# Modulation vectors of a layered model: summed along rows of transposed weights instead of across partitions

## The chip, the cores and the metric

One core of one Trainium2 chip runs the whole program as one launch. The metric is the device time of that core in microseconds (us). A difference is told as after against before.

## The reference, cut to what matters

A 256 x 1024 activation passes through a first block (gated recurrence, spatial gating, SwiGLU), then a gated linear attention layer ("GLA"), a retrieval layer ("PEER"), a sliding-window attention layer and a second PEER layer. Everything is float32. Each of these layers is modulated by vectors that depend on a conditioning vector `c` alone:

```python
mod = (jax.nn.silu(c) @ w_mod[l] + b_mod[l]).reshape(bsz, N_MOD, D_MODEL)      # first block, 6 parts
mod = c_act @ mod_w[l] + mod_b[l]                                              # two later layers, 6 parts each
sh1, sc1, g1, sh2, sc2, g2 = jnp.split(mod, 6, axis=-1)
kv_mod = c_act @ kv_mod_w + kv_mod_b                                           # 2 parts
h = rmsnorm(x, g) * (1.0 + scale) + shift                                      # shift, scale: parts 0, 1, 3, 4
x = x + gate * y                                                               # gate: parts 2 and 5
```

Each part is a vector of 1024 numbers, the product of a vector of 1024 and a 1024 x 1024 weight matrix (4 MB). The kernel computes 18 of the parts in the way that is changed here: parts 2 to 5 of the first block (key "m"), 0 to 5 of the two later layers ("m0", "m1") and two for the shared keys and values ("kv"). Parts 0 and 1 of the first block are made by other code (`mod_start`), which stays.

## The kernel before, in words

The weights of all layers stream from HBM as tiles of 128 x 1024 float32 (512 KB) into a ring of buffers called `raw`. `raw()` (L225) issues the load on the queue of SyncE (SP). For the layers, `halves()` splits each tile in two: ScalarE (ACT) copies it to a rounded type (`wh`, L268) and VectorE (DVE) subtracts (`wl`, L270). TensorE (PE) then makes three products for each block: `wh` by the activation's high part (L284 and its like), `wl` by the same (L285), `wh` by the low part (L286). There are 3 `wh` and 3 `wl` buffers, and some stages add more with `more()`. In PEER, 128 tiles of `peer_u` are multiplied first (L1617 to L1619), then 128 tiles of `peer_v` (L284 to L286), for which `acth` and `actl` are made as well (L1713, L1714).

The modulation parts are background work. `mod_part` is a generator that yields after each of its 8 weight tiles. `pump()` is called after every tile that `halves()` gives, and advances the generator by one unit each time its credit, raised by `s.rate` (0.2 to 0.75), reaches 1. `need()` runs a part to its end where a layer wants it, and `mod()` and `gate()` fetch it. A unit goes like this: one `raw` tile holds two row blocks of 512 columns, and DVE adds each, times its number of silu(c), to an accumulator:

```python
rj = r[:, j * 512:j * 512 + 512]
if k == 0:
    i = nc.vector.tensor_scalar(acc, rj, c[:, 0:1], None, op0=OP.mult)                                     # L383
else:
    i = nc.vector.scalar_tensor_tensor(acc, rj, c[:, k:k + 1], acc, op0=OP.mult, op1=OP.add)               # L385
```

After 4 units (half a part) the 128 partitions of `acc` (tile `modacc`, one buffer) hold partial sums. Four products with a vector of ones on PE (L391, 8 passes) sum them across the partitions into PSUM, DVE adds a bias (L395, tile `modsb`), GpSimd (POOL) writes the 512 numbers to a DRAM row (L397), and, for parts that are no gates, reads them back as columns (L399). POOL also loads the bias for each half (L376). Gates stay in DRAM until `gate()` loads them, repeated over 128 partitions, on SP. `scale_vec` (L550) is the first reader of the column form.

The order on each engine isn't the order of the code: the framework's planner places the instructions by its own costs and priorities, and adds the semaphores. An engine then runs its list in order, so that an instruction which waits holds up all behind it.

At the start, `warm()` (L328) runs 18 dummy products on a zeroed tile (`modbias`, L164) while the first loads land. In the GLA layer, L1183 multiplies the query with the running state of each chunk of 64 rows, with a tile of zeros as the state of the first chunk, and L1185 adds the product within the chunk.

Of the kernel before, what the change touches and what calls it, by code (L numbers as in the profile page):

```python
# [9 lines left out]
F32 = mybir.dt.float32  # L10
# [30 lines left out]
COLS = [("c", 8), ("cx", 8), ("c2", 8), ("g_mix", 8), ("g_ffn", 8), ("bm", 16), ("lb", 16), ("b_s", 4)]  # L41
COLS2 = [("ng", 32), ("kvg", 8), ("bg2", 4)]
# [69 lines left out]
class Prog:  # L112
    def __init__(s, ctx, tc, a):
# [15 lines left out]
        s.mid = False  # L129
# [24 lines left out]
    def setup(s):  # L154
# [3 lines left out]
        s.actp = s.pool("act", 1, side="right")  # L158
        s.early = s.pool("early", 1, side="right", ctx=s.ectx)
# [3 lines left out]
        s.modbias = s.t(c, [128, 128])  # L163
        nc.gpsimd.memset(s.modbias, 0.0)  # L164
# [20 lines left out]
        s.cvec = {"m": act, "m0": act2, "m1": act2, "kv": act2}  # L185
        s.part0 = {"m": 2, "m0": 0, "m1": 0, "kv": 0}
        s.modb0 = {"m": 0, "m0": 6, "m1": 12, "kv": 18}
        ones = s.t(c, [128, 1])
        nc.vector.memset(ones, 1.0)
        s.ones32 = ones.to_broadcast([128, 32])  # L190
# [169 lines left out]
    def mod_part(s, key, part):  # L360


        nc = s.nc
        w = s.a["w_" + key]
        c = s.cvec[key]
        s.uid += 1
        row = s.dram.tile([1, 1024], F32, name=f"mod{s.uid}")
        gate = part in (2, 5)
        if not gate:
            m = s.t(s.early if key == "m" else s.consts, [128, 8])  # L370
        for h in range(2):
            acc = s.t(s.stream, [128, 512], tag="modacc", bufs=1)
            s.mid = True
            i = s.modb0[key] + part
            bias = s.a["modb"][i:i + 1, h * 512:h * 512 + 512].rearrange("o (g c) -> (o g) c", g=4)
            nc.gpsimd.dma_start(s.modbias[0:128:32, :], bias)  # L376
            for q in range(4):
                r = s.raw(w[part - s.part0[key], h, q])
                for j in range(2):
                    k = 2 * q + j  # L380
                    rj = r[:, j * 512:j * 512 + 512]
                    if k == 0:
                        i = nc.vector.tensor_scalar(acc, rj, c[:, 0:1], None, op0=OP.mult)  # L383
                    else:
                        i = nc.vector.scalar_tensor_tensor(acc, rj, c[:, k:k + 1], acc, op0=OP.mult, op1=OP.add)  # L385
                    s.queue(i, 0)
                if q < 3:
                    yield
            p = s.ps("C", [128, 128])
# [3 lines left out]
            s.mid = False  # L393
            sb = s.t(s.stream, [128, 128], tag="modsb", bufs=1)
# [3 lines left out]
            if not gate:  # L398
                nc.gpsimd.dma_start(m[64 * h:64 * h + 64, :], rh.rearrange("o (p k) -> (o p) k", k=8))  # L399
            elif h:  # L400
                s.gates[key, part] = row
            if h:
                if not gate:
                    s.mods[key, part] = m
                s.done.add((key, part))
            yield
# [651 lines left out]
    def gla(s, x, first, after):  # L1058
        nc, a = s.nc, s.a
        fl = lambda t: t.rearrange("p a b -> p (a b)")  # L1060
        with ExitStack() as c1:
# [93 lines left out]
            s0 = s.t(p, [128, 4, 256])  # L1155
            nc.gpsimd.memset(s0, 0.0)
            st = {0: s0}
# [18 lines left out]
            for b in range(2):  # L1176
                for i in range(2):
                    po = s.ps("C", [128, 2, 256])
                    for j in range(2):
                        h = 2 * i + j  # L1180
                        for r in range(2):
                            ch = 2 * b + r
                            nc.tensor.matmul(po[64 * r:64 * r + 64, j], lhsT=qt[:, h, ch * 64:ch * 64 + 64],  # L1183
                                             rhs=st[ch][:, h], start=(j == 0), stop=False)
                        nc.tensor.matmul(po[:, j], lhsT=sc[b][:, h], rhs=v[:, b, h * 256:h * 256 + 256],  # L1185
                                         start=False, stop=(j == 1))
                    nc.scalar.activation(on[:, b, 2 * i:2 * i + 2], po, AF.Copy)
# [30 lines left out]
            s.rate = 0.0  # L1218
        return first
# [359 lines left out]
    def peer(s, l, x, first, after):  # L1579
# [4 lines left out]
        with ExitStack() as c1:  # L1584
# [105 lines left out]
            while s.mid:  # L1690
                s.pump_n(1)
# [5 lines left out]
            W0 = s.t(s.stream, [128, 2, 256], F32R, tag="modacc", bufs=1)  # L1697
            W1 = s.t(rl, [128, 2, 256], F32R, tag="RO", bufs=1)
# [4 lines left out]
            def parts_of(e):  # L1703

                if e not in made:
                    W = tile_of(e)
                    if e < 2:
                        Wh, Wl = W0[:, e], W1[:, e]
# [169 lines left out]
def layout(i):  # L1878
    d = {}
# [71 lines left out]
```

## Time and profile before

| | |
|---|---|
| median of 3 runs | 2409.5 us (2408.84 to 2420.38) |
| the profiled execution | 2407.28 us, of which the span of the profile is 2405.4 us |
| mean granted clock of TensorE | 0.995 |
| busy: PE, DVE, ACT, POOL | 97%, 78%, 48%, 3% |

The profile is of one execution, 2.2 us under the median of the runs. Busy is the time that an engine had an instruction in it, added up. A busy PE isn't PE at its peak, since matmuls are pipelined and their ends are modelled; starts are better to go by. Times in the rows count from the start of the span.

### The profile page before, as it was taken

How to read it: one execution, taken by the hardware profiler on the slowest of the kernel's cores; microseconds unless marked ns; L12 is line 12 of the kernel's file. 1: busy time of each engine (PE TensorE's matmuls, PEld its weight loads, DVE VectorE, ACT ScalarE, POOL GpSimd, SP SyncE). 2: the span in 40 equal slices, each digit the busy share in tenths (PEclk: the TensorE clock that was granted, in tenths of full speed). 3: DMA queues.
4: the chain of work that ended last, by engine and by line, in shares of the span. 5: the costliest groups of instructions: out<-in, count | busy, mean ns of one | idle time of the engine just before them, and what ended most of it. 6: DMA issues, size and time to landing. Idle time of an engine off the chain costs nothing. (4 is left out here: it accounts for less than half of the span.)

```text
span 2405.4 us, 40735 instructions
## 1 busy us (share of the span) xinstructions
PE 2335.6 (97%) x15652; PEld 2060.7 (86%) x15652; DVE 1871.4 (78%) x3521; ACT 1163.4 (48%) x1889; POOL 69.4 (3%) x123
## 2 busy tenths in 40 slices
PE   8999999999899999999999989999999999999998
PEld 6979789877799999997777777689999999888886
DVE  6678887887679989998777787658998999556665
ACT  5455454464454544445454445545454444445543
POOL 0000000000000000000000010000000000000000
PEclk9999999999999999999999999999999999999999
DMA  7438498745455544447778884244554444556763
GB/s 299 154 99 300 163 358 294 267 149 186 145 160 190 161 157 158 150 150 254 254 263 299 284 301 173 79 146 164 179 167 158 155 149 161 185 188 214 239 223 107
DMA packets 132898, 474.04 MB, mean 197 GB/s; under 512 B 17712, under 2 KB 18640, under 8 KB 131424
## 3 DMA queue, kind: packets, MB, share of 16 engines
q1 hardware_dynamic: 129632, 471.23, 58.2%
q8 instruction: 123, 2.02, 0.3%
q0 software_dynamic: 3072, 0.21, 0.1%
q14 instruction: 71, 0.58, 0.1%
HBM read 470.25 MB, written 1.12 MB: 196 GB/s over the span
## 5 line engine op out<-in xcount | busy, mean ns | idle before, releaser
L270 DVE TENSOR_TENSOR wl<-raw,wh 128x1024 fp32r<-128x1024 f32 x425 | 517.7, 1222 | 151.1 <-ACT wh L268 150.4
L268 ACT ACTIVATE wh<-raw 128x1024 fp32r<-128x1024 f32 x425 | 448.4, 1056 | 359.6 <-issue 120.6
L1617 PE MATMUL psB<-acth,wh 128*128 128x256 f32 x1776 | 505.1, 284 | 1.1 <-ACT u L1623 1.1
L1619 PE MATMUL psB<-acth,wl 128*128 128x256 f32 x1776 | 502.7, 283 | 0.0
L1618 PE MATMUL psB<-actl,wh 128*128 128x256 f32 x1776 | 500.2, 282 | 0.0
L284 PE MATMUL psA<-wh,acth 128*128 128x512 f32 x880 | 351.3, 400 | 3.0 <-ACT acth L570 2.3
L285 PE MATMUL psA<-wl,acth 128*128 128x512 f32 x880 | 350.6, 399 | 2.4 <-DVE wl L270 2.2
L286 PE MATMUL psA<-wh,actl 128*128 128x512 f32 x880 | 349.4, 397 | 1.0 <-DVE actl L571 1.0
L1617 PEld LDWEIGHTS psB<-acth,wh 128*128 128x128 f32 x1776 | 334.8, 188 | 1.5 <-ACT u L1623 1.5
L1618 PEld LDWEIGHTS psB<-actl,wh 128*128 128x128 f32 x1776 | 335.5, 189 | 0.0
L1619 PEld LDWEIGHTS psB<-acth,wl 128*128 128x128 f32 x1776 | 333.2, 188 | 0.2
L285 PEld LDWEIGHTS psA<-wl,acth 128*128 128x128 f32 x880 | 166.2, 189 | 46.0 <-DVE wl L270 6.7
L284 PEld LDWEIGHTS psA<-wh,acth 128*128 128x128 f32 x880 | 165.8, 189 | 46.0 <-ACT acth L570 2.8
L1713 ACT ACTIVATE acth<-u 128x256 fp32r<-128x256 f32 x240 | 97.3, 414 | 215.9 <-PE psA L285 215.7
L286 PEld LDWEIGHTS psA<-wh,actl 128*128 128x128 f32 x880 | 166.1, 189 | 41.2 <-DVE actl L571 1.4
L270 DVE TENSOR_TENSOR wlx<-raw,whx 128x1024 fp32r<-128x1024 f32 x116 | 141.5, 1222 | 42.4 <-ACT whx L268 42.1
L268 ACT ACTIVATE whx<-raw 128x1024 fp32r<-128x1024 f32 x116 | 122.0, 1054 | 98.7 <-PE psB L1618 30.3
L385 DVE SCALAR_TENSOR_TENSOR modacc<-raw,u,modacc 128x512 f32<-128x512 f32 x173 | 129.4, 748 | 39.1 <-DMA raw<-in_w_m 22.3
L1714 DVE TENSOR_TENSOR actl<-u,acth 128x256 fp32r<-128x256 f32 x240 | 99.6, 422 | 66.3 <-ACT acth L1713 66.3
L268 ACT ACTIVATE wh<-rawx 128x1024 fp32r<-128x1024 f32 x95 | 100.2, 1058 | 99.9 <-PE psB L1618 43.8
L270 DVE TENSOR_TENSOR wl<-rawx,wh 128x1024 fp32r<-128x1024 f32 x95 | 115.8, 1221 | 36.9 <-ACT wh L268 36.8
L268 ACT ACTIVATE whx<-rawx 128x1024 fp32r<-128x1024 f32 x86 | 90.6, 1058 | 87.7 <-DMA rawx<-in_w_up 17.6
(556 smaller groups left out, 4639.9 us busy)
## 6 DMA issues: line engine op xcount, KB each, us to landing
raw<-in_peer_u SPq DMA_DIRECT2D x212, 512.0 KB, 4.0
raw<-in_peer_v SPq DMA_DIRECT2D x209, 512.0 KB, 4.6
raw<-in_w_m SPq DMA_DIRECT2D x83, 512.0 KB, 5.1
rawx<-in_peer_v SPq DMA_DIRECT2D x47, 512.0 KB, 5.4
rawx<-in_w_m SPq DMA_DIRECT2D x45, 512.0 KB, 6.6
rawx<-in_peer_u SPq DMA_DIRECT2D x44, 512.0 KB, 4.0
raw<-in_w_in SPq DMA_DIRECT2D x27, 512.0 KB, 5.5
rawx<-in_w_up SPq DMA_DIRECT2D x25, 512.0 KB, 8.3
```

The costliest lines, as they stand in the source:

```text
L268: s.queue(nc.scalar.activation(wh, x, AF.Copy))
L270: s.queue(nc.vector.tensor_tensor(wl, x, wh.bitcast(F32), op=OP.subtract))
L284: mm(out, lhsT=lh, rhs=rh, start=start, stop=False)
L285: mm(out, lhsT=lh, rhs=rl, start=False, stop=False)
L286: mm(out, lhsT=ll, rhs=rh, start=False, stop=stop)
L385: i = nc.vector.scalar_tensor_tensor(acc, rj, c[:, k:k + 1], acc, op0=OP.mult, op1=OP.add)
L1617: mm(pu, lhsT=wh[:, sl], rhs=hT[:, k], start=(k == 0), stop=False)
L1618: mm(pu, lhsT=wh[:, sl], rhs=lT[:, k], start=False, stop=False)
L1619: mm(pu, lhsT=wl[:, sl], rhs=hT[:, k], start=False, stop=(k == 7))
L1713: nc.scalar.activation(Wh, W, AF.Copy)
L1714: nc.vector.tensor_tensor(Wl, W, Wh.bitcast(F32), op=OP.subtract)
```

## The change

A part's weights now lie transposed: partition p of tile k holds the 1024 weights of one output number. `silu(c)`, repeated over all partitions (tile `crow`), is multiplied with the tile along its row, and the same DVE instruction gives the row's sum (`accum_out`), which is the output number itself, already in column form. So each unit (still one 512 KB tile) has one DVE instruction over 128 x 1024 where there were two over 128 x 512. The products with ones, `modacc`, `modsb`, the bias loads, and for non-gates the way through DRAM are gone. The biases come with one larger load of column data at the start (160 columns more). Gates are written to a DRAM row by POOL, once for a part.

`crow` is loaded on SP (512 KB, from one row of DRAM) and put through Silu on ACT when the key changes between "m" and the others, and again after each PEER layer's first half, because its buffer then is the tile `L` of that layer. That makes four loads.

Three small things go with it: the tile for `warm()` is zeroed later in POOL's list, two tiles of the second half of PEER move from `modacc` and `RO` to `RO` alone, and GLA leaves out the product with the zero state, for which two products of 128 columns are split in two of 64.

```diff
@@ setup
-        s.modbias = s.t(c, [128, 128])
-        nc.gpsimd.memset(s.modbias, 0.0)
...
-        act2 = s.t(c, [128, 8])
-        nc.scalar.activation(act2, s.cols[0][:, 16:24], AF.Silu)
@@ warm
         p = s.ps("B", [128, 128])
+        z = s.t(s.startp, [128, 128])
+        s.nc.gpsimd.memset(z, 0.0)
         for _ in range(18):
-            s.nc.tensor.matmul(p, lhsT=s.modbias, rhs=s.modbias, start=True, stop=True)
+            s.nc.tensor.matmul(p, lhsT=z, rhs=z, start=True, stop=True)
@@ mod_part
+        if s.ckey != (key == "m"):
+            s.ckey = key == "m"
+            s.crow = s.t(s.crow_at[0], [128, 1024], tag=s.crow_at[1], bufs=1)
+            r = 0 if s.ckey else 1
+            nc.sync.dma_start(s.crow, s.a["crow"][r:r + 1, :].to_broadcast([128, 1024]))
+            nc.scalar.activation(s.crow, s.crow, AF.Silu)
...
-        for h in range(2):
-            acc = s.t(s.stream, [128, 512], tag="modacc", bufs=1)
...
-            nc.gpsimd.dma_start(s.modbias[0:128:32, :], bias)
-            for q in range(4):
-                r = s.raw(w[part - s.part0[key], h, q])
...
-            for g in range(4):
-                nc.tensor.matmul(p[32 * g:32 * g + 32, :], lhsT=s.ones32, rhs=acc[:, g * 128:g * 128 + 128],
-                                 start=True, stop=True, tile_position=(0, 32 * g))
...
-            nc.vector.tensor_tensor(sb, p, s.modbias, op=OP.add)
-            rh = row[:, h * 512:h * 512 + 512]
-            nc.gpsimd.dma_start(rh.rearrange("o (g c) -> (o g) c", g=4), sb[0:128:32, :])
-            if not gate:
-                nc.gpsimd.dma_start(m[64 * h:64 * h + 64, :], rh.rearrange("o (p k) -> (o p) k", k=8))
...
+        for k in range(8):
+            r = s.raw(w[part - s.part0[key], k])
+            s.queue(nc.vector.scalar_tensor_tensor(r, r, 1.0, s.crow, op0=OP.mult, op1=OP.mult,
+                                                   accum_out=m[:, k:k + 1]), 0)
+            if k < 7:
+                yield
+        nc.vector.tensor_tensor(m, m, s.col("mb", 8 * (s.modb0[key] + part), 8), op=OP.add)
+        if gate:
...
+            nc.gpsimd.dma_start(row.rearrange("o (p k) -> (o p) k", k=8), m)
@@ gla
+                        if b or j == 0:
+                            nc.tensor.matmul(po[:, j], lhsT=sc[b][:, h], rhs=vh, start=(j == 0), stop=False)
+                        else:
+                            for r in range(2):
+                                rs = slice(64 * r, 64 * r + 64)
+                                nc.tensor.matmul(po[rs, j], lhsT=sc[b][:, h, rs], rhs=vh, start=False, stop=(r == 0))
...
+                            if ch:
@@ peer
-            while s.mid:
-                s.pump_n(1)
...
-            W0 = s.t(s.stream, [128, 2, 256], F32R, tag="modacc", bufs=1)
-            W1 = s.t(rl, [128, 2, 256], F32R, tag="RO", bufs=1)
+            W01 = s.t(rl, [128, 2, 2, 256], F32R, tag="RO", bufs=1)
+            s.crow_at, s.ckey = (rl, "L"), None
```

## Rows read from the trace of the kernel before

**Rows 1.** The page, busy time of each engine over the whole span

```profile
PE 2335.6 (97%) x15652; PEld 2060.7 (86%) x15652; DVE 1871.4 (78%) x3521; ACT 1163.4 (48%) x1889; POOL 69.4 (3%) x123
```

**Rows 2.** Stretches: length, then each engine's busy time (instructions), clock, DMA share, GB/s

```profile
300.00:460.00 160.00, 158.31 (x1158) 146.55 (x1157) 127.60 (x156) 73.75 (x81) 11.50 (x20) 1.00 0.89 321
...
1236.00:1436.00 200.00, 188.91 (x866) 146.23 (x864) 157.13 (x241) 91.25 (x135) 16.32 (x29) 1.00 0.84 290
```

**Rows 3.** The same for L391 alone (8 passes a group): PE busy (passes)

```profile
300.00:460.00 160.00, 3.40 (x64) 1.00 0.89 321
...
1236.00:1436.00 200.00, 4.68 (x88) 1.00 0.84 290
```

**Rows 4.** Timeline of PE: start, length, what; around one group of L391 passes

```profile
138.33 0.39 PE L286 MATMUL psA<-whx,actl 128*128 128x512 f32 x1
...
138.65 0.42 PE L391 MATMUL psC<-modacc,u 128*32 128x128 f32 x8
...
139.00 0.50 PE L284 MATMUL psA<-whx,acth 128*128 128x512 f32 x1
...
139.34 0.39 PE L285 MATMUL psA<-wlx,acth 128*128 128x512 f32 x1
...
139.57 0.40 PE L286 MATMUL psA<-whx,actl 128*128 128x512 f32 x1
```

**Rows 5.** Tile modacc: PE idle before L391, by what ended it (us, times)

```profile
  DVE modacc L385: 5.4, 3
```

**Rows 6.** Waits of 1090 to 1440 us: total us, times, longest

```profile
ACT wh L268 <- DMA raw<-in_peer_v: 60.2, 41, 4.2
```

**Rows 7.** Waits of DVE over the span: total us, times, longest

```profile
DVE scalev L550 <- DMA u<-mod: 14.5, 5, 4.8
```

**Rows 8.** Timeline of DVE, end of the GLA layer

```profile
612.90 0.17 DVE L550 SCALAR_TENSOR_TENSOR scalev<-u,u 128x8 f32<-128x8 f32 x1 [4.37 <-DMA u<-mod]
```

**Rows 9.** Timeline of PE, end of the first block's mixers, and end of GLA

```profile
272.54 0.50 PE L286 MATMUL psA<-wh,o1l 128*128 128x512 f32 x1 [1.67 <-DVE o1l L946]
...
619.97 0.41 PE L521 MATMUL psB<-u,nb 128*128 128x128 f32 x2 [3.55 <-DVE nb L518]
```

**Rows 10.** Groups of DVE instructions, shapes apart: busy us, mean ns

```profile
L666 DVE TENSOR_TENSOR_SCAN w<-u,w 128x1024 f32<-128x1024 bf16 x1 | 2.3, 2283 | 0.0
...
L1106 DVE SCALAR_TENSOR_TENSOR w<-w,w 128x1024 f32<-128x1024 f32 x1 | 1.2, 1226 | 1.1 <-ACT w L1105 1.1
```

**Rows 11.** Timeline of DVE in the second half of the first PEER layer

```profile
1332.62 1.23 DVE L270 TENSOR_TENSOR wlx<-rawx,whx 128x1024 fp32r<-128x1024 f32 x1
1333.76 0.28 DVE L395 TENSOR_TENSOR modsb<-psC,u 128x128 f32<-128x128 f32 x1
...
1334.69 1.53 DVE L385 SCALAR_TENSOR_TENSOR modacc<-raw,u,modacc 128x512 f32<-128x512 f32 x2
1336.14 1.22 DVE L270 TENSOR_TENSOR wlx<-raw,whx 128x1024 fp32r<-128x1024 f32 x1
```

**Rows 12.** Groups of ACT instructions, shapes apart: busy us, mean ns

```profile
L470 ACT ACTIVATION_READ_ACCUMULATOR psA<-u 128x1 f32 x24 | 4.5, 188 | 0.0
...
L784 ACT ACTIVATE w<-w 128x1024 f32<-128x1024 f32 x2 | 2.1, 1062 | 3.8 <-DVE w L783 3.8
...
L990 ACT ACT_TABLE_LOAD x1 | 1.3, 1283 | 0.0
```

**Rows 13.** DMA issues: count, KB each, median us to landing

```profile
u<-in_rows SPq DMA_DIRECT2D x2, 512.0 KB, 6.3
```

**Rows 14.** Timeline of PE in the GLA layer, the zero state

```profile
549.03 1.08 PE L1183 MATMUL psC<-u,w 128*64 128x256 f32 x4
```

**Rows 15.** Timeline of the first 10 us

```profile
1.00 6.98 PE L328 MATMUL psB<-u 128*128 128x128 f32 x36 [1.00 <-POOL u L164]
1.17 0.13 POOL L171 IOTA u<- 128x1 f32 x1
...
9.08 1.07 PE L348 MATMUL psC<-mraw,u 128*32 128x256 f32 x16 [1.11 <-DVE u L179]
```

More of the change, by code (lines that the diff above doesn't have):

```diff
@@ L158, in setup @@
         s.actp = s.pool("act", 1, side="right")
+        s.mctx = ExitStack()
+        s.crow_at = s.pool("modp", 1, side="right", ctx=s.mctx), "crow"
         s.early = s.pool("early", 1, side="right", ctx=s.ectx)
@@ L363, in mod_part @@
         nc = s.nc
+        if s.ckey != (key == "m"):
[4 more added lines that the diff above has]
+            nc.scalar.activation(s.crow, s.crow, AF.Silu)
         w = s.a["w_" + key]
-        c = s.cvec[key]
-        s.uid += 1
-        row = s.dram.tile([1, 1024], F32, name=f"mod{s.uid}")
         gate = part in (2, 5)
-        if not gate:
+        if gate:
+            m = s.t(s.small, [128, 8], tag="mgate", bufs=2)
+        else:
@@ new lines, in mod_part @@
+        for k in range(8):
[5 more added lines that the diff above has]
+        nc.vector.tensor_tensor(m, m, s.col("mb", 8 * (s.modb0[key] + part), 8), op=OP.add)
+        if gate:
+            s.uid += 1
+            row = s.dram.tile([1, 1024], F32, name=f"mod{s.uid}")
+            nc.gpsimd.dma_start(row.rearrange("o (p k) -> (o p) k", k=8), m)
+            s.gates[key, part] = row
+        else:
+            s.mods[key, part] = m
@@ L408, in add_mods @@
+        s.done.add((key, part))
+        yield
     def add_mods(s, key, parts):
@@ L1880, in layout @@
     tok = lambda v: v.reshape(2, 128, 1024).transpose(1, 0, 2).reshape(128, 2048)
+    d["crow"] = np.stack([i["c"].reshape(-1), i["c_2"].reshape(-1)])
     d["x"], d["ctx"] = tok(i["x"]), tok(i["ctx"])
-    cols = {"c": _col(i["c"]), "cx": _col(i["c_ctx"]), "c2": _col(i["c_2"]), "g_mix": _col(i["g_mix"]),
+    cols = {"c": _col(i["c"]), "cx": _col(i["c_ctx"]), "g_mix": _col(i["g_mix"]),
             "g_ffn": _col(i["g_ffn"]), "bm": _col(i["b_mod"][0][:2048]), "ng": _col(i["norm_g_2"]),
             "kvg": _col(i["kv_norm_g_2"]), "lb": _col(i["lb_gamma"]), "b_s": i["b_s"][0].T, "bg2": _col(i["gla_b_g2_2"])}
+    mb = np.concatenate([i["b_mod"][0], i["mod_b_2"].reshape(-1), i["kv_mod_b_2"]]).reshape(20, 1024)
+    cols["mb"] = np.concatenate([b.reshape(128, 8) if p % 6 in (2, 5) else _col(b) for p, b in enumerate(mb)], axis=1)
     for n, c in enumerate((COLS, COLS2)):
@@ L1889, in layout @@
     d["rows"] = np.concatenate([rows[k].reshape(1, -1) for k, _ in ROWS], axis=1)
-    mb = np.concatenate([i["b_mod"][0], i["mod_b_2"].reshape(-1), i["kv_mod_b_2"]]).reshape(20, 1024)
-    d["modb"] = np.stack([b if p % 6 in (2, 5) else b.reshape(8, 128).T.reshape(-1) for p, b in enumerate(mb)])
     d["pos"] = i["positions_2"].reshape(2, 128).T
     d["w_s"] = i["w_s"][0].transpose(2, 0, 1)
-    def parts(w):
-        v = w.reshape(8, 128, -1, 1024).transpose(2, 0, 1, 3)
-        t = v.reshape(-1, 8, 128, 8, 128).swapaxes(3, 4).reshape(v.shape)
-        return [u.reshape(-1, 4, 2, 128, 2, 512).transpose(0, 4, 1, 3, 2, 5).reshape(-1, 2, 4, 128, 1024)
-                for u in (v, t)]
     def mods(w):
-        v, t = parts(w)
-        return np.stack([v[p] if p % 3 == 2 else t[p] for p in range(v.shape[0])])
+        t = w.T.reshape(-1, 1024, 1024)
+        return np.stack([v.reshape(128, 8, 1024).swapaxes(0, 1) if p % 3 == 2 else v.reshape(8, 128, 1024)
+                         for p, v in enumerate(t)])
     d["w_m01"] = (i["w_mod"][0][:, :2048].reshape(8, 128, 2, 4, 256).transpose(3, 2, 1, 0, 4)
```

49 lines of the change are left out of this document (10 added, 39 removed).

## The prediction

> **What bounds the kernel now.** I read the busy times of the page first [rows 1]: PE is busy 97% of the span, DVE 78%. So time that PE no longer spends is a gain nearly everywhere, and work of other engines counts where it stops PE. Then I read stretches [rows 2]. From 300 to 460 us (SwiGLU) PE is busy 158.3 of 160 us. From 1236 to 1436 us (the end of the first PEER layer, where the parts come fastest) it is busy 188.9 of 200, and DVE 157.1. There 11 us of PE are lost, and ACT waits a lot for `peer_v` tiles (41 waits, 60 us [rows 6]); their loads can only be issued when DVE has freed a buffer. That stretch hangs on DVE and on buffers as well as on PE.
>
> The view of PE's timeline around one group of the products with ones [rows 4] gives the main price. Products of 512 columns start 0.23 us apart (139.34 to 139.57). From the last such product (138.33) to the first one after the group (139.00) it is 0.67 us, which is 0.44 more than a step; and the next step is 0.34 in place of 0.23, as the pipeline fills again. A group thus costs PE 0.55 us.
>
> **What is removed.** *Groups on PE.* 18 parts of two halves have 36 groups of 8 passes, 19.8 us in all. 25 of them lie outside 1236 to 1436 us, and I credit them in full: 13.75 us. The 11 inside (88 passes [rows 3]) are 6.05 us; there DVE and the buffers may take the place of PE, so I credit half, 3.0, and keep 0 and 6.05 as bounds.
>
> *PE's waits for DVE's sums.* PE stood three times before a group because `modacc` wasn't done, 5.4 us [rows 5], all in that same stretch. With no group the wait goes. What is late next is the `wl` of the coming tile, made by the same DVE behind the same backlog. I take half, 2.7; bounds 0 and 5.4.
>
> *The way through DRAM.* For shift and scale, DVE waited five times for the read-back, 14.5 us [rows 7]. Two of them lie before a stall of PE. At the end of GLA, DVE stood 4.37 us until 612.90 [rows 8], with the residual of the first half of the tokens behind it; PE then stood 3.55 us until 619.97 for what came out of that residual [rows 9]. The residual's input was there earlier: the second half's 36 products of 0.23 us ended at 616.4 (619.97 less 3.55), so the first half's were done near 608.2. Without the wait the residual starts up to 4.4 us earlier, which covers the 3.55: I take 3.5. At the end of the mixers PE stood 1.67 us for a DVE result [rows 9] behind a wait of the same kind; I take 0.7 of it, since that result has other work ahead of it too. Sum 4.2; bounds 0 and 5.2.
>
> *GLA.* The zero state's four products are 8 passes; four took 1.08 us [rows 14], about 0.4 of it for the last one to end, so 0.22 from start to start: 1.7 us go. Two products are split in two, 4 passes more, 0.9 us. Net 0.9 us of PE.
>
> **What DVE does.** A unit is now two instructions; the pair at 1334.69 lets the next instruction start at 1336.14 [rows 11], 1.45 us. After, it is one instruction with two float32 inputs over 128 x 1024. The trace has one of the same operation and shape, without the row sum: 1226 ns [rows 10]; and a subtraction of that shape lets the next start after 1.14 us (1332.62 to 1333.76 [rows 11]). How the sum gets out isn't shown on DVE. On ACT, reading out such a sum is an instruction of its own of 188 ns [rows 12]. So a unit costs between 1.14 and 1.33, and DVE gains 0.1 to 0.3 us on each of 144 units. I book nothing for it, since PE sets the pace in most places; in 1236 to 1436 us it could bring up to 5.7 us, the part of PE's 11.1 idle us that isn't in the 5.4 above. That goes into the range.
>
> [...]
>
> **What is added.** `crow` is loaded four times. The nearest row is a 512 KB load of repeated rows, 6.3 us to landing [rows 13]. Then come Silu over 128 x 1024, 1.06 us like an Exp of that shape, and twice (after each PEER's Gelu) a table load of 1.28 us [rows 12]. On SP the load waits for the last reader of the old buffer, with weight loads queued behind it; on ACT the Silu waits for the landing, with the splits behind it; those feed DVE and PE. Cover: three `wh` tiles, which in `peer_v` are 12 products of 0.23 us each, 8.3 us against 8.6 for landing, table and Silu. In SwiGLU, where the keys change, seven more buffers are open. With the cover nothing is lost, without it 8.6 us each time, 34 in all. I take 2.0 us for the four, near the lower end, because the planner sees the wait and can place other work ahead of it. The longer column load at the start (82 KB more, a sixth of a 512 KB load) takes 0.3 us.
>
> Booked at nothing: zeroing the warm-up tile behind L171 instead of ahead of it. L171 ends at 1.30 us, so the 6.98 us of warm-up end near 8.4 instead of 8.0; the first real product starts at 9.08 and waits for DVE [rows 15], so 0.7 us of cover are left, and a later start would cost at most 0.4. POOL's 96 small transfers become 6, and PE waits for none of them. The two tiles moved to `RO` wait for the same last reader as one of them did before. `while s.mid` found nothing to do, as no part is begun in the first halves of PEER (rate 0).
>
> **Sum.** 13.75 + 3.0 + 2.7 + 4.2 + 0.9 = 24.55 us less, 2.3 more: 22.25 us less than the profiled execution's 2407.28, so 2385.0. That execution is 2.2 us under the median shown, so as a median 2387.2, told as 2387.
>
> **Rivals.** *Swallowed gains.* In 1236 to 1436 us the buffers, not PE, set the pace, so that neither the 3.0 nor the 2.7 appears; the residuals at the layers' ends wait for something else (no 4.2); and one reload of `crow` is exposed (8.6). Then 14.65 - 8.9 = 5.75 us are left: 2404. For it: ACT's 60 us of waits for tiles [rows 6]. Against it: most groups lie where PE is busy without a gap. Chance 0.18.
>
> *DVE at half rate.* The row sum makes the engine take two steps for each element, as a running scan over 1024 elements does in this trace (2283 ns [rows 10]). With 0.1 for reading out, a unit is 2.38 us, 0.93 more. 300 to 460 us has 32 units (8 groups of 4 [rows 3]) and DVE would need 127.6 + 29.8 = 157.4 of 160 us; 1236 to 1436 has 44, 157.1 + 40.9 = 198.0 of 200. If DVE can be kept busy 90% there, the stretches grow by 15 and 20 us, and the gains in them (4.4 and 5.7) are lost: 2409.5 + 35 - 12.1 = 2432. It comes out slower if DVE can't be kept busy over 95.5% there (355.4 / 0.955 is 12 us more than 360); before, its share was 79 to 80% [rows 2]. Against it: the same instruction without the sum runs at one step an element. Chance 0.08.
>
> *Exposed reloads.* All four `crow` loads stop SP and ACT without cover: 34.4 in place of 2.0, so 2387 + 32 = 2419. It turns slower from 24.3 us of exposed time on. Against it: three tiles of cover and the planner's placing. Chance 0.04.
>
> **Chances and range.** The forecast with its bounds (gain of 12 us or more) has 0.70. About 0.5% (12 us) is what a measurement of this kernel can tell from no change. Faster by more than that: 0.70 and 0.05 from the fast edge of the first rival, 0.75. Within it: 0.13 of that rival and 0.01 of the others, 0.14. Slower: 0.11 from the last two. The low end has all upper bounds: 19.8 + 5.4 + 5.2 + 0.9 + 5.7 - 0.3 = 36.7, so 2373. The high end reaches most of the first rival, 2401. The forecast's own range is 2373 to 2397.
>
> **What would show it.** No L391, L395 and `modacc` in the profile; products on PE 0.23 us apart where groups stood, and PE's busy time 15 to 20 us lower with fewer gaps. DVE's unit at 1.2 to 1.3 us with a read-out behind it; 2.3 would be the half rate. `scalev` without a DMA wait, and PE's gap near 620 us gone. The prediction is wrong if ACT or SP stands for several us at a load of `crow`, if PE stands for `wl` in the late stretch where it stood for `modacc`, or if the planner, given other costs, orders the layers' ends worse.

## Result, and the profile after

The changed kernel took 2373.8 us (median of 4 runs, 2370.9 to 2376.0) beside 2412.7 us of the kernel before on the same chip: a ratio of 0.983, with a 95% interval of 0.980 to 0.986. On the 2409.5 us of the prediction that is 2369.5 us. Faster was right. The size was too small: 22 us were forecast, some 40 came, and 2369.5 us lies 3.5 us below the low end of the range.

The profiled execution took 2370.9 us, span 2369.1, which is 36.3 us less than the span of before, at a mean granted clock of 0.992 where the profile of before had 0.995. First the page's busy times, as in [rows 1]:

```profile
PE 2302.0 (97%) x15360; PEld 2043.0 (86%) x15360; DVE 1846.0 (78%) x3502; ACT 1174.3 (50%) x1897; POOL 16.3 (1%) x32
```

PE is busy 33.6 us less. DVE is busy only 25 us less, and its share stays at 78%. The stretches that answer to [rows 2]; they lie 4 to 10 us earlier in SwiGLU, and 18 to 32 us earlier at the end of the first PEER layer:

```profile
296.00:450.00 154.00, 151.83 (x1089) 142.91 (x1088) 124.83 (x159) 72.89 (x82) 1.09 (x2) 1.00 0.93 349
1218.00:1404.00 186.00, 181.57 (x777) 144.80 (x776) 151.56 (x242) 94.20 (x136) 0.88 (x2) 1.00 0.89 312
```

In the second, PE idles 4.4 us where it was 11.1 in 200 us. Then DVE's timeline there, which answers to [rows 11]: the new unit, its read-out, and the instruction behind it.

```profile
1309.26 1.22 DVE L374 SCALAR_TENSOR_TENSOR raw<-raw,L 128x1024 f32<-128x1024 f32 x1
1310.40 0.08 DVE L374 DVE_READ_ACCUMULATOR raw<-raw,L 128x1 f32 x1
1310.40 1.22 DVE L264 TENSOR_TENSOR wl<-raw,wh 128x1024 fp32r<-128x1024 f32 x1
```

A unit is 1.22 us, as the same operation without a sum was [rows 10]. The read-out of 0.08 us starts 1.14 us after the unit, and the next instruction starts with it: it costs DVE nothing that shows. So DVE runs this unit no slower than without a sum, and 1.14 us from start to start is the low end of what the prediction gave.

Last, PE at the end of GLA, in place of the 3.55 us of [rows 9]:

```profile
604.48 0.41 PE L502 MATMUL psB<-u,nb 128*128 128x128 f32 x2 [0.50 <-DVE nb L499]
```

Where the time came from follows from the start of the same PE instruction in two traces. The table gives the change of that difference over each stretch, in us (minus: the later trace gains). "Again" is a further execution of the same kernel (e14 and e0 below), and shows how far a number can be trusted. Entries are rounded one by one.

| stretch, us of the trace before | forecast | changed | changed again | before again |
|---|---|---|---|---|
| 0 to 250, mixers (5 groups) | -2.5 | +2.1 | +2.5 | +1.4 |
| 250 to 274, end of mixers (1 group) | -1.3 | -4.9 | -4.9 | -0.2 |
| 274 to 490, SwiGLU (9 groups) | -5.0 | -9.5 | -9.6 | +4.3 |
| 490 to 600, GLA (2 groups, zero state) | -2.0 | +0.6 | +3.8 | -1.6 |
| 600 to 664, end of GLA (1 group) | -4.1 | -6.3 | -5.7 | +0.1 |
| 664 to 1085, 1600 to 2035: `peer_u` | 0 | -6.2 | -6.3 | +0.1 |
| 1085 to 1446, first `peer_v` (16 groups) | -8.5 | -11.5 | -8.7 | +2.8 |
| rest (2 groups) | -1.1 | -1.0 | -1.9 | +1.1 |
| four loads of `crow` | +2.0 | in the above | | |
| sum | -22.3 | -36.6 | -30.8 | +7.9 |

The forecast's 25 groups outside the late stretch, its 8.45 for `peer_v` (five of the 25, 3.0, 2.7) and its other terms are put where they belong; its 0.3 for the column load (an estimate: 82 KB at the 290 to 321 GB/s of [rows 2]) is in the first row. Three rows miss by more than executions differ: the two ends, where the way through DRAM stood, and `peer_u`, in which the change does nothing. In the first row the gain of five groups is missing.

Part of these rows is the clock granted to PE, which the profile gives for each stretch as a mean share of full speed. Here are the two ends in the kernel before, in the columns of [rows 2] (the clock is the third number from the end), and two products in the second of them:

```profile
270.00:277.00 7.00, 5.33 (x17) 3.89 (x16) 5.72 (x9) 0.63 (x1) 0.00 (x0) 0.76 0.50 167
620.00:625.00 5.00, 4.14 (x16) 3.36 (x17) 4.57 (x14) 2.69 (x6) 1.04 (x1) 0.66 0.01 2
...
622.77 0.63 PE L284 MATMUL psA<-whx,u 128*128 128x512 f32 x1
623.20 0.63 PE L285 MATMUL psA<-wlx,u 128*128 128x512 f32 x1
```

After the gaps of [rows 9] PE ran on at a lower clock for a while (0.53 from 273.5 to 276.5 us, 0.50 from 622 to 624.5): products of 512 columns start 0.43 us apart there, in place of 0.23. A share of 0.76 over 7 us, or of 0.66 over 5 us, is by an estimate from these shares 1.7 us of full-speed work lost at each end. The clock of the changed kernel doesn't fall at these places, but does so twice in the mixers, the first time after PE stood for DVE:

```profile
262.00:277.00 15.00, 15.00 (x66) 11.80 (x66) 11.77 (x16) 5.62 (x8) 0.00 (x0) 1.00 0.45 141
604.00:610.00 6.00, 5.52 (x28) 4.70 (x29) 4.76 (x11) 2.89 (x7) 1.05 (x1) 1.00 0.07 22
...
110.00:120.00 10.00, 6.94 (x47) 6.95 (x47) 8.18 (x11) 6.19 (x9) 0.00 (x0) 0.83 0.50 154
190.00:200.00 10.00, 9.05 (x62) 8.29 (x61) 10.00 (x19) 6.08 (x8) 0.00 (x0) 0.83 0.65 220
...
113.06 1.81 PE L771 MATMUL psB<-u,w 128*128 128x128 f32 x8 [4.23 <-DVE w L766]
```

The last two stretches have 1.00 in both executions of the kernel before, and 0.83 in both of the changed kernel. That is 3.4 us lost, which is more than the 2.8 us of the five groups. All four profiles of kernels with the way through DRAM fall at both ends (before with 0.76 and 0.66, e2 below with 0.77 and 0.81, and e0 and e5); none of the other fourteen does at either (1.00 and 1.00 in the changed kernel).

In these four profiles the clock is also most of what two executions of one kernel differ by. They have 0.995 and 0.991 (before, again) and 0.992 and 0.990 (changed, again). If PE is taken as the bound throughout, which is an estimate, that is 12, 22, 19 and 24 us lost. At full clock the spans would be 2393 and 2392 us before, 2350 and 2351 us after.

### The profile page after: what moved, and what is told of

It is laid out like the page before. It is cut to its first block, busy times and chain, and to the rows that moved or that the text cites. A ratio compares the mean times of both kernels' runs of the same rounds, so it can differ in the third digit from the quotient of the medians.

```text
span 2369.1 us, 39891 instructions
## 1 busy us (share of the span) xinstructions
PE 2302.0 (97%) x15360; PEld 2043.0 (86%) x15360; DVE 1846.0 (78%) x3502; ACT 1174.3 (50%) x1897; POOL 16.3 (1%) x32
## 3 DMA queue, kind: packets, MB, share of 16 engines
HBM read 472.30 MB, written 1.07 MB: 200 GB/s over the span
## 5 line engine op out<-in xcount | busy, mean ns | idle before, releaser
L374 DVE SCALAR_TENSOR_TENSOR raw<-raw,L 128x1024 f32<-128x1024 f32 x61 | 74.7, 1224 | 60.7 <-DMA raw<-in_w_kv 30.1
```

The lines of the kernel that those rows point to most:

```text
L374: s.queue(nc.vector.scalar_tensor_tensor(r, r, 1.0, s.crow, op0=OP.mult, op1=OP.mult, accum_out=m[:, k:k + 1]), 0)
```

## Experiments

**The kernel before, once more.** No edit.

> The kernel before, unchanged, profiled a second time. In the profile of before the first stretch of peer_u products lasts 409.9 us from its first product to its last, after the change 406.8, and the second 409.7 and 407.1, though nothing of the change lies in them; products of 256 columns start 120 ns apart at the median before and 117 after. Theory A: executions, or chips, differ by that much whatever the kernel; then this profile has a stretch away from 409.9 by 1 us or more, up or down. Theory B: the change made these products faster (tiles at other addresses, fewer small transfers); then this profile has 409.9 and 409.7 again, within 0.5.

2415.2 us. The two `peer_u` stretches, from first to last start, took 410.2 and 410.0 us in this one run, as before (410.2 and 409.9), while the changed kernel's are 407.0 and 407.4. So these 6 us are no chance of one execution.

**Groups back.** The eight passes per group, on constant data, without the waits:

```diff
+            if k % 4 == 3:
+                pz = s.ps("C", [128, 128])
+                for g in range(4):
+                    nc.tensor.matmul(pz[32 * g:32 * g + 32, :], lhsT=s.ident[:, 0:32], rhs=s.ident,
+                                     start=True, stop=True, tile_position=(0, 32 * g))
```

> After the change, with the 36 groups of 8 passes on PE put back as products of the identity tile that nothing reads and that wait for nothing (the output is that of the reference). Theory A, PE is the bound and a group costs 0.55 us: 19.8 us slower than after the change (2373.8), so about 2393.5, with the loss spread evenly. Theory B, the gain came from waits between DVE, DMA and PE that the products brought with them, and PE has slack where they stood: under 8 us slower, below 2382.

2392.6 us, ratio to before 0.992 (0.990 to 0.994): 18.8 us over the changed kernel, 0.52 us a group. The price of 0.55 from [rows 4] holds. From 1085 to 1446 us this kernel is 1.1 us ahead of the first trace of before, the changed kernel 11.5 and 8.7: 7.6 to 10.4 us for 16 groups, so there they cost their full price too.

**The way through DRAM back.** Shift and scale go out and come in again:

```diff
         else:
-            s.mods[key, part] = m
+            row = s.dram.tile([1, 1024], F32, name=f"mod{s.uid}")
+            rv = row.rearrange("o (p k) -> (o p) k", k=8)
+            nc.gpsimd.dma_start(rv, m)
+            m2 = s.t(s.early if key == "m" else s.consts, [128, 8])
+            nc.gpsimd.dma_start(m2, rv)
+            s.mods[key, part] = m2
```

> After the change, with shift and scale parts sent through a DRAM row again by POOL (one write, one read back for a part) before their first reader. Theory A, the wait for the read-back stood in front of the residuals at the ends of GLA and of the first block's mixers and cost PE 9 us there (the lag between the two traces jumps by 5.5 and 5.2 us at these places, 0.55 and 1.1 of it from groups): 6 to 11 us slower, with DVE waiting for a DMA in front of scale_vec again. Theory B, these two jumps came from another order that the planner chose: less than 3 us slower.

2395.2 us, ratio 0.993 (0.991 to 0.995): 21.4 us over the changed kernel, against an expected 6 to 11. DVE's waits in this kernel (total us, times, longest), then two rows of its timeline, and PE's wait behind the second:

```profile
DVE scalev L537 <- DMA u<-mod: 24.8, 5, 7.7
```

```profile
259.57 0.17 DVE L537 SCALAR_TENSOR_TENSOR scalev<-u,u 128x8 f32<-128x8 f32 x1 [5.85 <-DMA u<-mod]
...
604.18 0.17 DVE L537 SCALAR_TENSOR_TENSOR scalev<-u,u 128x8 f32<-128x8 f32 x1 [3.42 <-DMA u<-mod]
...
618.88 0.41 PE L508 MATMUL psB<-u,nb 128*128 128x128 f32 x2 [3.95 <-DVE nb L505]
```

The end of the mixers gives back 6.2 us and the end of GLA 5.0, together more than the 4.2 that the prediction had for both. The clock is part of it, as it falls at both ends again:

```profile
260.00:275.00 15.00, 12.06 (x49) 9.51 (x48) 11.80 (x15) 4.53 (x6) 0.00 (x0) 0.77 0.27 79
616.00:625.00 9.00, 6.12 (x24) 5.13 (x25) 6.62 (x19) 3.26 (x8) 0.87 (x1) 0.81 0.00 0
```

These are 3.4 and 1.7 us lost. Another 6.9 go from 1085 to 1446 us (4.1 against the other execution of the changed kernel). Over the whole run the clock is 0.986, against 0.991 in the runs of the changed kernel: by the same estimate some 12 of the 21.4 us are PE at the lower clock, and the other 9 lie within what was expected. The run overstates what was removed: here both halves of a part travel after its last unit, while before the first half travelled earlier (24.8 us of waits against 14.5 [rows 7]).

**A longer unit.** A small instruction of DVE behind each unit:

```diff
+            s.queue(nc.vector.tensor_tensor(r[:, 0:128], r[:, 0:128], r[:, 128:256], op=OP.mult), 0)
```

> After the change, with one more DVE instruction of 128 x 128 behind each of the 144 multiply-and-sum instructions, about 0.2 us, so that a unit takes about 1.4 us as before the change in place of 1.2. The vectors are not changed by it. Theory A, DVE's shorter units gave the late part of the first PEER layer what the sum left out (9 us beyond its groups): 4 to 10 us slower, in the stretch that was 1243 to 1446 us before. Theory B, DVE's unit has no part in it and the waits went because no product waits for a sum: under 2 us.

2373.6 us, ratio 0.983 (0.981 to 0.986): no change that these runs can tell, though each of 144 units is followed by 0.29 us of DVE. A unit longer by that much costs nothing that shows.

**The mutual waits of before.** The kernel before with all groups and transfers, but without DVE waiting for the groups and PE for the sums; shift, scale and gate hold wrong values:

```diff
-                nc.tensor.matmul(p[32 * g:32 * g + 32, :], lhsT=s.ones32, rhs=acc[:, g * 128:g * 128 + 128],
+                nc.tensor.matmul(p[32 * g:32 * g + 32, :], lhsT=s.ones32, rhs=s.ident,
...
-            nc.vector.tensor_tensor(sb, p, s.modbias, op=OP.add)
+            nc.vector.tensor_tensor(sb, acc[:, 0:128], s.modbias, op=OP.add)
```

> The kernel before, with all its groups of products with ones and all its transfers, but without the mutual waits: the groups read a constant tile in place of the sums, and the tile that is sent to DRAM is made from the sums directly (so shift, scale and gate hold wrong values). Theory A (in the late stretch of the first PEER layer the change saved more than the groups because DVE waited for a group queued on TensorE and TensorE for DVE's sums): the stretch from 1288 to 1446 us gets some 8 to 12 us shorter, and the time is 8 to 14 us under the kernel before (ratio 0.994 to 0.9965). Theory B (these waits overlapped with others): within 3 us of the kernel before.

2402.9 us, ratio 0.997 (0.995 to 0.998): 9 us less, inside what the first theory expected. Here is the late stretch in three kernels, in the columns of [rows 2]: before, uncoupled, changed.

```profile
1250.00:1446.00 196.00, 183.88 (x833) 142.50 (x832) 156.91 (x237) 92.31 (x134) 16.32 (x29) 0.99 0.85 293
```

```profile
1255.00:1440.00 185.00, 182.87 (x836) 142.74 (x837) 156.22 (x238) 92.65 (x133) 16.81 (x29) 1.00 0.88 311
```

```profile
1232.00:1413.00 181.00, 176.38 (x754) 140.31 (x753) 147.66 (x231) 93.79 (x134) 0.88 (x2) 1.00 0.89 313
```

PE idles 12.1, 2.1 and 4.6 us. Without the mutual waits 10 us of PE's idle time in that stretch are gone; [rows 5] show one side of them, 5.4 us, and DVE's side is in its waits before:

```profile
DVE modsb L395 <- PE psC L391: 12.2, 6, 3.8
```

But half of what the late part gains (12.5 us from 1300 to 1446) is lost just ahead of it (6.7 from 1110 to 1250), as in the changed kernel (3.7, of which 1.7 is a clock of 0.83 from 1180 to 1190). So from 1085 to 1446 us this kernel is 5.5 us ahead of the first trace of before. e1 has groups without these waits too and is 1.1 us ahead there: what the waits cost in that stretch is between the two.

**A buffer for the modulation tiles.** They leave the ring (three weight buffers remain) and have one buffer, loaded one unit ahead:

```diff
-        r = s.ring("raw", F32, 4)
+        r = s.ring("raw", F32, 3)
...
+    def own(s, ap):
+        r = s.t(s.stream, [128, 1024], tag="modw", bufs=1)
+        s.nc.sync.dma_start(r, ap)
+        return r
```

> The changed kernel, with one buffer of its own for the modulation tiles, taken from the weight ring (three left), and each tile's load issued one unit ahead of its multiply-and-sum. Theory A (the multiply-and-sum waits for its own tile's landing with the weight split queued behind it on DVE, and that lost the 6 us from 1098 to 1243 us): DVE's waits for those tiles fall from 88 us in all to under 30, that stretch gets 4 to 6 us shorter, and the time is 3 to 6 us under the changed kernel. Theory B (the ring of four is what keeps the loads ahead, and three are too few): the same or up to 10 us longer, with more waits of ACT for tiles.

2433.5 us, ratio 1.009 (1.007 to 1.012): 60 us over the changed kernel, worse than either theory gave. The waits of DVE that it was to end became longer (75 us for `raw` tiles in the changed kernel):

```profile
DVE raw L374 <- DMA raw<-in_w_m: 45.3, 32, 4.5
DVE raw L374 <- DMA raw<-in_w_kv: 30.1, 15, 3.9
```

```profile
DVE modw L380 <- DMA modw<-in_w_m: 136.5, 86, 4.5
...
DVE modw L380 <- DMA modw<-in_w_kv: 17.4, 15, 2.8
```

With a single buffer the next tile can be loaded only when the unit before it has read the last: of the units of `w_m` alone, 86 waited for their tile, 1.6 us on average. The time goes where units follow one another: 23 us between 455 and 485 us of the changed kernel's time, and 23 more between 1400 and 1462. PE stands there and then runs at a lower clock; here is the worst stretch, at 0.50:

```profile
480.00:490.00 10.00, 1.66 (x4) 0.84 (x4) 7.86 (x11) 0.74 (x2) 0.00 (x0) 0.50 0.37 104
```

The clock of the whole run is 0.978, against 0.991: by the estimate used above, some 32 of the 60 us. So it says that four shared buffers are better than three and one; whether the waits in the changed kernel cost anything it doesn't tell. The same instructions lost 3.7 us from 1110 to 1250 us in one execution and 0.5 in that of e4, whose clock there is 1.00, so that loss is mostly one of executions.

**Zeros first.** The warm-up's tile is zeroed at the head of POOL's list again:

> The changed kernel with the warm-up tile zeroed at the head of GpSimd's list again, as before. The planner then places the copies of the first modulation products ahead of the first weight split on ACT again. Theory A (the 2.1 us lost in the first 15 us come from ACT standing 4.4 us for the first weight tile with those copies behind it): the first weight products start 2 us earlier against the changed kernel, and the time is 1.5 to 3 us lower, if no later order changes. Theory B (the start is set by the longer column load or by the transfers): no change there.

2372.4 us, ratio 0.984 (0.982 to 0.985): 1.4 us less, no difference that can be told. In the changed kernel the planner had put the first weight split of ACT ahead of a copy that PE needs:

```profile
13.24 1.06 ACT L262 ACTIVATE wh<-raw 128x1024 fp32r<-128x1024 f32 x1 [4.38 <-DMA raw<-in_w_in]
14.20 0.37 ACT L348 ACTIVATE modsb<-psC 128x256 f32<-128x256 f32 x1
```

```profile
14.62 1.02 PE L350 MATMUL psC<-u,modsb 128*128 128x2 f32 x4 [2.54 <-ACT modsb L348]
```

The copy's input was ready near 9.9 us (the 16 passes of L344, 1.07 us from 8.86 on), and the copy ran at 14.20, behind the split and its wait of 4.38 us. With zeros first PE has that copy 4 us earlier:

```profile
10.69 0.51 PE L351 MATMUL psC<-u,modsb 128*128 128x2 f32 x4
```

The order came back, and yet by 40 us only 0.6 of the 2.2 us were regained; the kernel before itself, run again, was 1.4 us later there. So the edit that was booked at nothing did change the order, at a price that can't be told from the difference of two executions.

**Where the buffers lie.** The change took tiles out of SBUF and put others in, which moved the weight rings: the first `wh` started 896 bytes past a multiple of 1024, and now starts at one. (These places are those that the framework gave the tiles; the traces hold no addresses, and what the runs vary is the length of the padding.) An unused tile moves them back, or elsewhere:

```diff
+        s.pad = s.t(c, [128, 224])
+        nc.vector.memset(s.pad[:, 0:1], 0.0)
         s.ident = s.t(c, [128, 128])
```

> The changed kernel with one unused tile of 896 bytes in the constants, so that all buffers behind it (the weight rings and the activations) start at the same place within 512 bytes as in the kernel before; instructions and their order stay. In the kernel before each of the two stretches of peer_u products took 409.8 us, in the changed kernel and the three variants of it so far 406.6 to 407.2. Theory A (the place of the operands in SBUF makes the 256-column products slower or faster): both stretches go back to 409 to 410 us, and the time rises by about 5.5 us. Theory B (something else of the program, such as the instruction stream): both stay at 406.6 to 407.2, time within 2 us of the changed kernel.

> As the kernel with the old offsets, but with 256 bytes in place of 896. The first wl and wh tiles then start 256 bytes past a multiple of 1024. So far: 0, 512 and 320 past gave 407.0 to 407.4 us for the two peer_u stretches, 896 past gave 409.9 to 410.2. Theory A (only places near a multiple of 1024 from below are slow): 407 us. Theory B (places that are no multiple of 512 are slow, and the one at 320 is an exception): 409 to 410 us.

With 896 bytes: 2380.3 us (one run), `peer_u` 409.9 and 410.0 us, as before. With 256: 2372.7 us (one run), 407.0 and 407.1. First and last product of the first stretch, changed kernel and old offsets:

```profile
658.14 0.28 PE L1603 MATMUL psB<-acth,wh 128*128 128x256 f32 x1
...
1065.16 0.27 PE L1605 MATMUL psB<-acth,wl 128*128 128x256 f32 x1
```

```profile
662.42 0.28 PE L1605 MATMUL psB<-acth,wh 128*128 128x256 f32 x1
...
1072.30 0.29 PE L1607 MATMUL psB<-acth,wl 128*128 128x256 f32 x1
```

But for one small write to the unused tile the instructions are the same, and only the addresses differ. Then the activation tiles `acth` and `actl`, which in all these kernels start 992 bytes past a multiple of 1024, were moved:

```diff
+        s.pad = s.t(s.pool("pad", 1, side="right"), [128, 248])
         s.actp = s.pool("act", 1, side="right")
```

> The changed kernel with an unused tile of 992 bytes ahead of the two activation tiles, so that these start at a multiple of 1024 bytes (in all kernels so far at 992 past one); the weight rings stay where they are. The two stretches of peer_u products took 407.0 and 407.4 us. Theory A (the products gain from operands that start at such multiples, weights and activations alike): both stretches fall by a further 2 us or more, and the time by 4 us or more. Theory B (only the place of the weight rings, or their place relative to something else, matters): both stay within 0.6 us, the time within 2 us of the changed kernel.

2368.5 us, ratio 0.981 (0.979 to 0.982). Theory A was half right: the time fell by 5 us, but `peer_u` got slower (409.2 and 409.4). What gained is the last `peer_v` layer, where the same tiles hold the stationary operand: its products of 512 columns start every 226.7 ns on average (1000 of them, from the 50th on), and every 233.0 in the changed kernel. Together with the zeros in the gap:

> A candidate for the fastest version: the changed kernel with the activation tiles at a multiple of 1024 bytes, and with the warm-up's zeros at the head of GpSimd's list, kept in the tile that fills the gap. If both theories A (place of the activations; order at the start) hold: 5 us or more under the changed kernel, ratio to the kernel before 0.981 or lower. If neither holds: within 2 us of the changed kernel, 0.983 to 0.985.

2373.8 us, ratio 0.983 (0.981 to 0.984), with `peer_u` and `peer_v` as in e8: nothing added, and the 5 us that e8 had gained in time aren't there. Why is not shown.

> The changed kernel with the activation tiles 512 bytes past a multiple of 1024 (480 bytes unused ahead of them), rings as in the changed kernel (first tiles at a multiple of 1024). Before this run, activations minus rings (modulo 1024) and the first peer_u stretch were: 992, 480, 672, 736 with 407.0 to 407.4 us; 96 with 409.9; 0 with 409.2. And the 512-column products of the last peer_v layer took 233 ns with the activations at 992, and 226.7 with them at 0. Theory A (peer_u is slowed when moving and stationary tiles lie at nearly the same place modulo 1024, and peer_v by activation tiles that don't start at a multiple of 512): peer_u 407, peer_v 226.7, and the time 8 to 12 us under the changed kernel. Theory B (peer_u needs the activations away from a multiple of 512, peer_v wants them at 1024 only): peer_u 409, peer_v 233, the time 3 to 5 us above the changed kernel.

> The changed kernel with the activation tiles at a multiple of 1024 and the rings 256 bytes past one. Theory A (as in the run before this): peer_u 407, peer_v 226.7, and the time 8 to 12 us under the changed kernel, the fastest so far. Theory B (activations at a multiple of 1024 slow peer_u wherever the rings lie): peer_u 409.2, peer_v 226.7, the time 3 to 6 us under the changed kernel.

2371.9 us, ratio 0.982 (0.980 to 0.984), and 2370.1 us, 0.982 (0.981 to 0.984). Both have `peer_u` at 409.2 to 409.4 us and `peer_v` at 226.7 ns. So the place of activations and rings to each other doesn't decide it (at 512 `peer_v` gained too, which the second theory of e12 denied); in these runs each use goes by the place of the activations. That rings moved alone slow `peer_u` too (e4) stands beside it. The changed kernel beside them:

> The changed kernel once more, on the same chip and beside the two, for a direct comparison: 2371 to 2376 us, peer_u 407.0 to 407.4, peer_v 233.

2377.8 us (2369.6 to 2380.7), ratio 0.985 (0.983 to 0.987), `peer_u` 406.9 and 407.4, `peer_v` 233.0: its time in two sets of runs thus differs by 4 us, while these stretches agree to 0.1. Last, the two uses of the tiles are set 32 bytes apart:

```diff
+    def act_tiles(s, still=False):
+        h = s.t(s.actp, [128, 2056], F32R, tag="acth", bufs=1)
+        l = s.t(s.actp, [128, 2056], F32R, tag="actl", bufs=1)
+        h = h[:, 8:2056] if still else h[:, 0:2048]
+        l = l[:, 0:2048] if still else l[:, 8:2056]
...
+            WH, WL = s.act_tiles(True)
```

> The changed kernel with 32 spare bytes in each activation tile: where the activations are the moving operand of peer_u and the stationary one of the dense layers they start at 992 and 32 bytes past a multiple of 1024, and where the same tiles hold the stationary operand of peer_v they start at a multiple of 1024. Theory A (each operand counts by its own place: moving tiles of 256 columns are slow at multiples of 512, stationary tiles are slow elsewhere): peer_u 407.0 to 407.4 us, the last peer_v layer 226.7 ns a product, and the time 8 to 11 us under the changed kernel, 2364 to 2368. Theory B (what slows one of them is the place of both tiles together): one of the two stays slow, and the time is that of the runs with moved activations, 2368 to 2372, or above.

2369.6 us (2364.0 to 2371.1), ratio 0.981 (0.979 to 0.983). `peer_u` took 407.2 and 407.6 us, and `peer_v` 227.2 ns a product: both fast, so the first theory holds, though the time is 1.6 us above what it gave. (The clock of this profile is 0.989, that of the changed kernel 0.992; over the whole layer a product took 229.0 ns, and 227.9 in e8.) 230 us inside that layer, in the columns of [rows 2], for the changed kernel and this one:

```profile
2010.00:2240.00 230.00, 230.00 (x989) 185.02 (x988) 142.76 (x178) 116.80 (x174) 0.00 (x0) 1.00 0.63 206
```

```profile
2016.00:2246.00 230.00, 230.00 (x1014) 190.01 (x1013) 146.58 (x182) 119.95 (x178) 0.00 (x0) 1.00 0.66 213
```

PE counts as fully busy in both, at full clock, and gets through 25 more products. This version and that of e8 have the lowest ratios of all, 4 to 5 us under the changed kernel's first runs.

**Reloads.** `crow` is loaded for each of the 18 parts, not four times (`if True:` in place of the test of `s.ckey`):

> The changed kernel with the row loaded, and its Silu computed, anew for each of the 18 parts instead of four times in all. Theory A (these loads are hidden: in the changed kernel none of the four left a jump in TensorE's times): within 4 us of the changed kernel. Theory B (a load costs what the prediction booked without cover, up to 8.6 us, or half of it): 14 loads more make it 30 to 120 us longer.

2376.1 us, ratio 0.984 (0.982 to 0.985), between the two medians of the changed kernel. ACT's Silu rows (total us and mean ns; idle before them):

```profile
L365 ACT ACTIVATE L<-L 128x1024 f32<-128x1024 f32 x9 | 9.5, 1060 | 20.1 <-DMA L<-in_crow 20.1
L365 ACT ACTIVATE crow<-crow 128x1024 f32<-128x1024 f32 x9 | 9.5, 1054 | 0.0
```

ACT stands 20 us for them, and the time of the program shows nothing of it: fourteen more reloads cost no more than the 4 us by which two sets of runs of the changed kernel differ.

## Why the prediction was right in direction and short in size

*Groups.* The price was right: 0.55 us forecast, 0.52 measured over all 36 (e1). That the pipeline fills again behind a group was the author's reading; the rows show the longer step, 0.34 us in place of 0.23. Wrong was half credit for the eleven of the late stretch. "DVE and the buffers may take the place of PE" didn't happen: e1 gives back 7.6 to 10.4 us for the 16 groups from 1085 to 1446 us, and their full price is 8.8.

*PE's waits for DVE's sums.* 2.7 us were credited from one side of the wait. e5 shows what it was: DVE waits for a group queued on PE, PE for DVE's sums. Without both, PE's idle time there falls from 12.1 to 2.1 us, and the net gain from 1085 to 1446 us is 5.5 (1.1 by e1). Of the 11.5 and 8.7 us of that stretch in two executions, 8.5 were forecast: the row came out near, with groups credited too low; the waits' own share isn't fixed better than 1 to 5 us. That the gain comes late and some is lost ahead of it was not foreseen.

*The way through DRAM.* This term was mis-sized most among those that the prediction had: 4.2 us, of which 3.5 at the end of GLA and 0.7 at the end of the mixers. Measured, each less its one group: 5.2 to 5.8 and 4.3, about 10 us; and e2 puts 11.2 back at the two places. The step that failed is reading the worth of a wait from the one PE gap behind it. A second gap went at each place, and with the gaps the lower clock that followed them, for which the prediction had no term. At the end of GLA the gap of 3.55 us became 0.50, another of 0.86 went, and so did 1.7 us of lower clock, 5.6 us in all. At the mixers' end two gaps went, 1.67 and 1.21 (the prediction took 0.7 of the first alone), and 1.7 us of lower clock, 4.6 us, of which 1.1 fall after 274 us into the row of SwiGLU. Two rows of before show the second gaps:

```profile
264.66 0.50 PE L284 MATMUL psA<-whx,o0h 128*128 128x512 f32 x1 [1.21 <-ACT o0h L945]
...
621.46 0.66 PE L521 MATMUL psB<-u,nb 128*128 128x128 f32 x2 [0.86 <-DVE u L1268]
```

*Nothing for what the change doesn't touch.* The prediction had no term for `peer_u`. 6.2 us came from there, because the change moved the weight rings (e4 moves them back and leaves the rest of the change). This is the largest single miss, no row of the trace before could have shown it, and it is a gain of the new addresses, not of the new sum.

*Too much.* The five groups of the mixers (2.75 us) and 2.0 us in GLA don't appear. In the mixers the changed kernel has a wait of PE for DVE of 4.23 us, where from 90 to 215 us no wait of the kernel before is longer than 1.7, and falls twice to a lower clock (0.83 over 10 us each, 3.4 us). These take back what the groups gave. That the planner's new order brought them is likely, but not shown. With the groups back e1 is hardly later at 250 us (2.4 us behind the first trace, the changed kernel 2.1), but e1 falls only once there (1.00 from 190 to 200 us), 1.7 us in its favour. GLA's row differs by 3 us between two executions of the same kernel, so its 0.9 for the zero state can't be judged. Of these 3 us, 1.7 are the clock (0.83 in one and 0.66 in the other from 495 to 505 us). The 2.0 us for reloads were not needed (e10); the table load of 1.28 us, which the prediction had before two of the four Silus, stands before three of them in the profile after.

*Rivals.* DVE at half rate falls: a unit takes 1.22 us with the sum, and the same operation took 1.23 without it [rows 10]. "Two steps" and "one step an element" were the author's reading of the scan's 2.28 us and of this 1.23. Swallowed gains did not come true in the late stretch, for which it was argued; in the mixers a gain is missing, by another way. Exposed reloads fall with e10.

*Open.* SwiGLU's row (-9.5) has 4.5 us beyond its groups. 1.1 of them are the clock after the mixers' end. 2.5 come from 460 to 490 us and recur, at 2.0 to 2.5, in the variants of the changed kernel that keep its buffers; the kernel before, run again, differs by 4.3 in the other direction, and no run isolates it.

## What to carry to other kernels

A change that adds or removes tiles can move the others, as it moved the weight rings here, which was worth 6.2 us. Where PE is busy without a gap, compare the step of products that the change doesn't touch before you credit the change, and try a padding tile of some hundred bytes. A wait isn't worth the one gap behind it (5.6 us went here with a gap of 3.55): look for further gaps, and at the granted clock of the stretch that follows, before you book it. The cost of the mutual wait of two engines couldn't be read from the waits of one of them (5.4 us here, where 10 us of idle time went and 1 to 5 us of time); it is measured by feeding each side from data that is ready.

## What the runs showed of the hardware that was not expected

In these runs the step of float32r products depended on where their operands start in SBUF, at a granted clock of 1.00 and with PE counted as busy. In `peer_u` (256 moving columns) a stretch took 406.9 to 407.6 us; it took 409.2 to 409.4 when the moving tile started at a multiple of 512 bytes (e8, e12, e13), and 409.9 to 410.2 with the rings 896 bytes past a multiple of 1024 (before, e4). In `peer_v` (512 columns) the step was 226.7 ns with the stationary tile at a multiple of 512 bytes and 233.0 with it 992 bytes past one of 1024; 233.8 with the rings at 896 too. The bytes are places as the framework gave them, moved by padding. What in the chip does this, no run shows.

A wait of PE cost more than its length here: behind gaps of 3.55 and 0.86 us the granted clock was 0.66 over 5 us, 1.7 us more, and gone with the gaps (1.00 in the changed kernel).

Reading out a row sum on DVE took 0.08 us and started together with the next instruction (both at 1310.40); the multiplication with a sum over 128 x 1024 float32 took 1.22 us, and 1.23 without one [rows 10].
